# Two layers on one core: the second layer's products with the values gathered into one run for each unit of attention

## The chip, the cores and the metric

The kernel runs on 1 core of one Trainium2 chip. The metric is the device time of one execution in microseconds, as the median of several runs.

## The reference, cut to what matters

Two transformer-like layers work on 1024 tokens of width 1024, all in fp32. The change lies in the second layer, in its attention with a forget gate (16 heads of 64, blocks of 128 queries, causal):

```python
fcum = jnp.cumsum(log_f, axis=-1)
for blk in range(seqlen // ATT_BLOCK):
    q0, q1 = blk * ATT_BLOCK, (blk + 1) * ATT_BLOCK
    s = jnp.einsum('bhqd,bhkd->bhqk', q[:, :, q0:q1], k[:, :, :q1]).astype(jnp.float32) * scale
    s = s + fcum[:, :, q0:q1, None] - fcum[:, :, None, :q1]
    s = jnp.where(kpos[None, :] <= qpos[:, None], s, -jnp.inf)
    prob = jax.nn.softmax(s, axis=-1)
    outs.append(jnp.einsum('bhqk,bhkd->bhqd', prob.astype(v.dtype), v[:, :, :q1]))
...
y_att = (o.astype(f32) * jax.nn.silu(z_att.astype(f32))).astype(x.dtype)
```

Around it stand the projections q, k, v and z_att of the layer's input with the weight `w_in_2`, a state-space branch, two gates, two branch products and an output product.

## The kernel before, in words

**Stages.** The first layer runs first. The second layer opens with projections and the state-space chunks (function `ssd`), and then comes the stage in question: attention, interleaved with the rest of the projections (q, k, v, the attention's gate z, the two branch gates) and with the state-space branch's products. In the profile this stage goes from about 1731 to 2541 us. The attention branch's products, the output product and the last norm follow.

**A unit of attention.** Heads go in pairs p = 0 to 7. Each pair has four units, u = 0 to 3, and a unit has a long and a short block of 128 queries, blocks 7 - u and u, which together always have 9 blocks of keys. A block's keys are taken two at a time; such a step is a *part* (p, i, kp), so that every unit has five parts: four with two blocks of keys and one with a single one. Four functions work on this:

- `scores` (L1551) makes one block's probabilities for one head: GpSimd adds the causal mask to a row of decays (L1560), TensorE multiplies queries and keys (L1568, L1569, tile `S`), VectorE adds and takes the running minimum (L1574), ScalarE takes the exponential (L1580), VectorE the reciprocal (L1582) and the scaling (L1588). Long blocks' probabilities lie in buffers of the pool `pg` (21 buffers of 4 KB for each partition), short ones' in `hp` (9 buffers of 2 KB).
- `tr` (L1594) transposes a part's probabilities for both heads on TensorE into a PSUM tile `pT` (L1600, two buffers), and copies them to a tile `pf` in `hp`: on VectorE for kp = 1 (L87), else on ScalarE (L89).
- `pv` (L1606) multiplies a part with the values (L1617). The two heads' outputs lie at PSUM partitions 0 to 63 and 64 to 127, so that each product takes half of the array's columns. One PSUM tile (`V`, one buffer) holds both of a unit's outputs, at columns 0 and 256. Behind a block's last part VectorE multiplies the output with the gate z (L1626); behind block 3, which is the last of a pair's, SyncE (SP) stores the pair's result to `scr["ya"]` (L1630), and for p = 6 two loads of it follow (`load_T`, L1686).
- `attention` (L1540) sets the order. For each part it issues `tr`; then, as soon as three parts are waiting, the oldest one's `pv`; then one of the four `scores` jobs of the next unit. The list of waiting parts goes on from one unit to the next.

The lines of that loop:

```python
            for i in blocks:
                for kp in range(i // 2 + 1):
                    yield tr(p, i, kp)
                    todo.append((p, i, kp))
                    if len(todo) >= 2 + 1:
                        for _ in range(1):
                            yield pv(*todo.pop(0))
                    if jobs:
                        job = jobs.pop(0)
                        scores(*job)
                        yield 0.107 * (job[1] + 1)
```

**The order around it.** `attention` is a generator; each `yield` gives the TensorE time that the author reckons for what was issued. `interleave` (L255) runs it as the main stream and, after each of its yields, issues batches of the other stream (`until`, L1719: the weight products) until that one has come as far by its own reckoning. A batch is six matmuls of 512 columns (L166, L167, L168, from `gemm_ch`), reckoned as 1.3 us; a task of the other stream is reckoned as 10.5 us, a unit of attention as 6.3 us (L1764 and the lines behind). All other weight products of this stage have the full array's columns (128\*128 in the profile), as have the scores and the transposes. Each engine then works through its queue in order. All loads and stores of this stage go through SP's queue.

Of the kernel before, what the change touches and what calls it, by code (L numbers as in the profile page):

```python
# [10 lines left out]
ALU = mybir.AluOpType  # L11
AX = mybir.AxisListType

P = 128
# [1088 lines left out]
def second_tasks():  # L1103

    tasks = []
    for g in range(4):
        tasks += [("x0", XS + g * 256, g), ("x1", XS + g * 256 + P, g), ("B", BM + g * P, g),
                  ("C", CM + g * P, g), ("z0", Z_SSM + g * 256, g),
                  ("z1", Z_SSM + g * 256 + P, g)]
    gates = [("gate", c0 + m * P, (gi, m)) for gi, c0 in enumerate((GS, GA)) for m in range(8)]  # L1110
    for p in range(8):
        tasks += gates[2 * p - 2 + (p > 5):2 * p + (p > 4) + (p > 5)] if p else []
        tasks += [("q", QO + p * P, p), ("k", KO + p * P, p)]
        if p % 2 == 0:
            tasks += [("v", VO + p * P, (p, ks)) for ks in ((0, 4), (4, 8))]
        tasks += [("za", ZA + p * P, p)]
    return tasks


def second_layer(cx, I, hT, late, scr, out):  # L1120
    nc = cx.nc
    tt = nc.vector.tensor_tensor
# [121 lines left out]
    As = [{} for _ in range(8)]  # L1244
# [295 lines left out]
    def attention():  # L1540

        units = [(p, (7 - u, u)) for p in range(8) for u in range(4)]
        fcs, st, parts, acc = {}, {}, {}, {}

        def load_fc(p):
            for e in range(2):
                fcs[e] = cx.pg("fc")
                h = 2 * p + e
                cx.bcast_row(fcs[e], scr["fc"][h * 8:h * 8 + 8, :].rearrange("c l -> (c l)"))

        def scores(p, i, e):  # L1551
            A = As[p]
            q, kk, kl, fc = A["q"][e], A["kk"][e], A["kl"][e], fcs[e]
            qs = slice(i * P, i * P + P)
            W = (i + 1) * P

            pt = cx.pg("prob") if i > 3 else cx.hp("prob")
            nc.gpsimd.tensor_tensor(out=pt[:, qs], in0=fc[:, qs], in1=cx.pos_q, op=ALU.add)  # L1560
            m = cx.st("m")
            top = BIG
            mi = 0
            for n0 in reversed(range(0, W, 512)):
                n1 = min(W, n0 + 512)
                S = cx.ps("S", "S")
                o = S[:, :n1 - n0]
                nc.tensor.matmul(o, q[:, qs], kk[:, n0:n1], start=True, stop=False)  # L1568
                nc.tensor.matmul(o, q[:, qs], kl[:, n0:n1], start=False, stop=True)  # L1569
                ranges = [(n0, n1, fc)] if n1 < W else [(i * P, W, pt), (n0, i * P, fc)]  # L1570
                for a, z, x in ranges:
                    if a == z:
                        continue
                    nc.vector.tensor_tensor_reduce(  # L1574
                        out=pt[:, a:z], in0=x[:, a:z], in1=S[:, a - n0:z - n0], scale=1.0,
                        scalar=top, op0=ALU.add, op1=ALU.min, accum_out=m[:, mi:mi + 1])
                    top = m[:, mi:mi + 1]
                    mi += 1
            rs = cx.st("rs")[:, 0:1]
            nc.scalar.activation(pt[:, :W], pt[:, :W], AF.Exp, bias=top, scale=-1.0,  # L1580
                                 accum_out=rs)
            nc.vector.reciprocal(rs, rs)  # L1582
            how = "dve"
            if how == "act":
                nc.scalar.activation(pt[:, :W], pt[:, :W], AF.Copy, scale=rs)
            else:
                eng = nc.gpsimd if how == "pool" else nc.vector
                eng.tensor_scalar(out=pt[:, :W], in0=pt[:, :W], scalar1=rs, scalar2=None,  # L1588
                                  op0=ALU.mult)
            st[p, i, e] = pt  # L1590

        def tr(p, i, kp):  # L1594
            t = cx.ps("T", "pT")
            n = min(2, i + 1 - 2 * kp)
            for e in range(2):
                for x in range(n):
                    kt = 2 * kp + x
                    nc.tensor.transpose(t[:, (n * e + x) * P:(n * e + x + 1) * P],  # L1600
                                        st[p, i, e][:, kt * P:(kt + 1) * P], cx.ident)
            f = parts[p, i, kp] = cx.hp("pf")
            cx.evac(f[:, :2 * n * P], t[:, :2 * n * P], kp in (1,))
            return 0.214 * n

        def pv(p, i, kp):  # L1606
            A = As[p]
            if i > 3 and kp == 0:
                acc[0] = cx.ps("V", "o")
            c = 0 if i > 3 else 256  # L1610
            o = acc[0][:, c:c + P]
            f = parts.pop((p, i, kp))
            n = min(2, i + 1 - 2 * kp)
            for x in range(n):
                kt = 2 * kp + x
                for e in range(2):
                    m = nc.tensor.matmul(o[e * 64:e * 64 + 64], A["v"][:, kt, e],  # L1617
                                         f[:, (n * e + x) * P:(n * e + x + 1) * P],
                                         start=kt == 0, stop=kt == i, skip_group_check=True)
                    if kt == 0 and e == 0:  # L1620
                        cx.after(m, acc.get("last"))
            acc["last"] = m
            cx.trail.append(m)
            if 2 * kp + n > i:
                z = A["z"][:, i * P:i * P + P]
                tt(out=z, in0=o, in1=z, op=ALU.mult)  # L1626
                for e in range(2):
                    st.pop((p, i, e))
                if i == 3:
                    nc.sync.dma_start(scr["ya"][p * P:(p + 1) * P, :], A["z"])  # L1630
                    A.clear()
                    if p == 6:
                        load_T(yaT, scr["ya"], 0, [6])
            return 0.269 * n

        todo = []
        jobs = []

        def next_jobs(n):
            p, blocks = units[n]  # L1640
            return [(p, i, e) for i in blocks for e in range(2)]

        load_fc(0)
        for job in next_jobs(0):
            scores(*job)
            yield 0.107 * (job[1] + 1)
        for n, (p, blocks) in enumerate(units):
            if n + 1 < len(units):
                if units[n + 1][0] != p:
                    yield None  # L1650
                    load_fc(p + 1)
                jobs = next_jobs(n + 1)
            for i in blocks:
                for kp in range(i // 2 + 1):
                    yield tr(p, i, kp)
                    todo.append((p, i, kp))
                    if len(todo) >= 2 + 1:
                        for _ in range(1):
                            yield pv(*todo.pop(0))
                    if jobs:  # L1660
                        job = jobs.pop(0)
                        scores(*job)
                        yield 0.107 * (job[1] + 1)
        for a in todo:
            yield pv(*a)

    def segment(gen):
        for dt in gen:
# [17 lines left out]
    def load_T(dst, src, b, ks=range(8)):  # L1686
        for k in ks:
            nc.sync.dma_start(dst(k, b)[1].bitcast(F32), src[k * P:(k + 1) * P, halves[b]])
# [25 lines left out]
    todo = [(kind, what) for kind, _, what in second_tasks()] + [("ssm", m) for m in range(8)]  # L1714
# [46 lines left out]
    interleave((until(marks[0]), 43.0), (chain(delayed(first[1], 1.0), dts), 32.0))  # L1761

    att = attention()
    for n in range(12):  # L1764
        rest = until(marks[n + 1])
# [45 lines left out]
    for n in range(4):  # L1811
        w = cx.weights()
        s = slice(n * 256, n * 256 + 256)
        for i in range(8):
            o = cx.ps("GSGSS"[i % 5], "out2")
# [7 lines left out]
            if n == 3:  # L1823
                ss = cx.st("ss")
                nc.vector.tensor_reduce(out=ss[:, 0:1], in_=sso[:, 4 * i:4 * i + 4], axis=AX.X,
                                        op=ALU.add)
# [103 lines left out]
```

## Time and profile before

| what | value |
|---|---|
| median of 3 runs | 2739.56 us (2738.61 to 2741.25) |
| the profiled execution's own time | 2741.01 us |
| its span, first to last instruction | 2738.9 us |
| TensorE busy (PE) | 2671.0 us |
| VectorE busy (DVE) | 1558.8 us |
| ScalarE busy (ACT) | 1015.2 us |
| GpSimd busy (POOL) | 386.4 us |

PE is TensorE's matmuls, PEld its loads of weights, which overlap with matmuls. Matmuls are pipelined: the next one starts before the one ahead has ended, so that what one costs the queue is read from the starts of neighbours and not from its duration. The bracket at the end of a row of the timeline is the idle time of the engine ahead of it and what ended it; "issue" is a wait for nothing that the profile shows. PEclk is the granted share of TensorE's full clock. A letter q behind an engine's name (SPq) is its instruction queue.

### The profile page before, as it was taken

The page shows a single profiled execution, that of the slowest core. Times are in us where ns is not written, and L with a number is a line of the kernel's source. Part 1 is how long each engine was busy: PE and PEld are TensorE (multiplying, and loading weights), DVE is VectorE, ACT ScalarE, POOL GpSimd, SP SyncE. Part 2 cuts the span into 40 slices and gives each one's busy share as a digit, 9 for nine tenths or more (in the row PEclk, how much of TensorE's full clock was granted, in tenths as well). Part 3 has the DMA queues.
Part 4 walks back from the last instruction along what each step waited for, and adds up shares of the span by engine and source line. Part 5 has one row for each costly group of instructions (what it writes and reads, how often), then busy time and mean ns, then how long its engine had stood idle before and what let it go on. Part 6 is the DMA issues. An engine that isn't in the chain of part 4 may idle for free. (4 is left out here: it accounts for less than half of the span.)

```text
span 2738.9 us, 38386 instructions
## 1 busy us (share of the span) xinstructions
PE 2671.0 (98%) x15391; PEld 2199.6 (80%) x15391; DVE 1558.8 (57%) x2857; ACT 1015.2 (37%) x1753; POOL 386.4 (14%) x368
## 2 busy tenths in 40 slices
PE   5999999999999999999899999999999999999999
PEld 5998667988888888887677778778778778777899
DVE  6645776665555555556577786544544444574443
ACT  4434775152222222233443443433433333352222
POOL 2211211421111100003011222200010000010000
PEclk9999999999999999999999999999999999999999
DMA  7111213321111111121133223222222222253533
GB/s 246 45 55 39 71 42 112 112 74 54 50 52 47 46 47 47 47 56 74 48 103 106 85 87 99 80 75 62 56 76 58 62 89 55 63 195 104 173 125 118
DMA packets 225438, 221.56 MB, mean 81 GB/s; under 512 B 15108, under 2 KB 173420, under 8 KB 225260
## 3 DMA queue, kind: packets, MB, share of 16 engines
q1 hardware_dynamic: 224608, 218.60, 26.0%
q8 instruction: 121, 1.98, 0.3%
q10 hardware_dynamic: 652, 0.51, 0.1%
q14 instruction: 57, 0.47, 0.1%
HBM read 180.67 MB, written 34.21 MB: 78 GB/s over the span
## 5 line engine op out<-in xcount | busy, mean ns | idle before, releaser
L79 ACT CAST wh<-land 128x1024 fp32r<-128x1024 f32 x163 | 170.9, 1050 | 550.5 <-PE up L167 345.1
L81 DVE TENSOR_TENSOR wlo<-land,wh 128x1024 fp32r<-128x1024 f32 x161 | 208.6, 1297 | 278.6 <-ACT wh L79 278.3
L166 PE MATMUL up<-h2h,wh 128*128 128x512 f32 x704 | 274.0, 390 | 0.7 <-DVE y L1022 0.7
L167 PE MATMUL up<-h2l,wh 128*128 128x512 f32 x704 | 274.1, 389 | 0.0
L168 PE MATMUL up<-h2h,wlo 128*128 128x512 f32 x704 | 273.9, 389 | 0.0
L1580 ACT ACTIVATE prob<-prob,m 128x128 f32<-128x128 f32 (+7 forms) x128 | 99.4, 776 | 259.4 <-DVE m L1574 258.8
L1006 DVE TENSOR_TENSOR x<-dn,x 128x512 f32<-128x512 f32 x176 | 119.2, 688 | 75.5 <-PE dn L168 75.5
L166 PE MATMUL ag<-h3h,wh 128*128 128x512 f32 x384 | 161.1, 420 | 0.0
L103 POOL TENSOR_TENSOR rstd<-ms,mhalf 128x1 f32<-128x1 f32 (+3 forms) x58 | 75.9, 1309 | 572.8 <-DVE ms L101 572.8
L1560 POOL TENSOR_TENSOR prob<-fc,consts 128x128 f32<-128x128 f32 x128 | 63.9, 514 | 657.0 <-PE pT L1600 364.3
L89 ACT COPY pf<-pT 128x512 f32<-128x512 f32 (+1 forms) x208 | 114.2, 559 | 112.3 <-PE pT L1600 74.4
L166 PEld LDWEIGHTS up<-h2h,wh 128*128 128x128 f32 x704 | 132.2, 188 | 28.4 <-issue 1.1
L167 PEld LDWEIGHTS up<-h2l,wh 128*128 128x128 f32 x704 | 132.2, 188 | 27.9 <-DVE h2l L228 0.4
L168 PEld LDWEIGHTS up<-h2h,wlo 128*128 128x128 f32 x704 | 132.1, 188 | 27.4
L992 POOL TENSOR_TENSOR wdf<-wdf,gate 128x512 f32<-128x512 f32 x44 | 73.0, 1682 | 568.9 <-DMA wdf<-in_w_down_dram 557.2
L168 PE MATMUL ag<-h3h,wlo 128*128 128x512 f32 x384 | 151.0, 393 | 0.0
L167 PE MATMUL ag<-h3l,wh 128*128 128x512 f32 x384 | 150.7, 392 | 0.0
L166 PE MATMUL dn<-wdh,gh 128*128 128x512 f32 x352 | 138.2, 393 | 1.7 <-DVE x L1006 1.4
L167 PE MATMUL dn<-wdl,gh 128*128 128x512 f32 x352 | 137.3, 390 | 0.0
L168 PE MATMUL dn<-wdh,gl 128*128 128x512 f32 x352 | 137.1, 390 | 0.0
L1574 DVE CUSTOM_DVE_ANT_0 prob<-prob,S 128x128 f32<-128x128 f32 x128 | 36.7, 287 | 175.6 <-PE S L1569 166.5
L166 PE MATMUL tok<-wh,h1h 128*128 128x256 f32 x448 | 130.4, 291 | 2.9 <-ACT h1h L226 2.9
(348 smaller groups left out, 7096.5 us busy)
## 6 DMA issues: line engine op xcount, KB each, us to landing
land<-in_w_in_dram SPq DMA_DIRECT2D x87, 512.0 KB, 3.9
wada<-in_w_ada_dram SPq DMA_DIRECT2D x96, 256.0 KB, 3.5
land<-in_w_up_dram SPq DMA_DIRECT2D x44, 512.0 KB, 4.0
wdf<-in_w_down_dram SPq DMA_DIRECT2D x44, 256.0 KB
scr_g<-gt SPq DMA_DIRECT2D x34, 256.0 KB, 2.3
x<-in_x_dram SPq DMA_DIRECT2D x16, 512.0 KB, 5.7
land<-in_w_out_dram SPq DMA_DIRECT2D x16, 512.0 KB
dab<-scr_da SPq DMA_DIRECT2D x32, 256.0 KB, 4.2
```

What stands on the lines that cost most here:

```text
L79: i = self.nc.scalar.copy(hi, src)
L81: eng.tensor_tensor(out=lo, in0=src, in1=hi.bitcast(F32), op=ALU.subtract)
L89: self.nc.scalar.copy(dst, src)
L103: self.nc.gpsimd.tensor_tensor(out=r[:, :width], in0=t[:, :width], in1=self.mhalf[:, :width], op=ALU.pow)
L166: i = mm(out, lh, rh, start=first, stop=False, **kw)
L167: mm(out, lh, rl, start=False, stop=False, **kw)
L168: self.last = mm(out, ll, rh, start=False, stop=last, **kw)
L992: nc.gpsimd.tensor_tensor(out=f, in0=f, in1=gt2[:, s], op=ALU.mult)
L1006: tt(out=x2[i][:, s], in0=o, in1=x2[i][:, s], op=ALU.add)
L1560: nc.gpsimd.tensor_tensor(out=pt[:, qs], in0=fc[:, qs], in1=cx.pos_q, op=ALU.add)
L1574: nc.vector.tensor_tensor_reduce(out=pt[:, a:z], in0=x[:, a:z], in1=S[:, a - n0:z - n0], scale=1.0, scalar=top, op0=ALU.add, op1=ALU.min, ...
L1580: nc.scalar.activation(pt[:, :W], pt[:, :W], AF.Exp, bias=top, scale=-1.0, accum_out=rs)
```

## The change

The products leave the loop over the parts. A unit now issues its five `tr` with the next unit's `scores` jobs between them, and behind the last one `values` issues all five `pv` of the unit (36 instructions) without a yield between them; then `gated` issues the gate's multiplications for the long and for the short block and, where there is one, the store. One yield with the sum of the reckoned times follows (2.4 us), and only then the interleaving goes on. Nothing is left waiting from one unit to the next. The products, their operands and their PSUM columns are the same.

```diff
--- before.py
+++ after.py
@@ -1621,19 +1621,29 @@
                         cx.after(m, acc.get("last"))
             acc["last"] = m
             cx.trail.append(m)
-            if 2 * kp + n > i:
+            return 0.269 * n
+
+        def gated(p, blocks):
+
+            A = As[p]
+            for i in blocks:
+                c = 0 if i > 3 else 256
                 z = A["z"][:, i * P:i * P + P]
-                tt(out=z, in0=o, in1=z, op=ALU.mult)
+                tt(out=z, in0=acc[0][:, c:c + P], in1=z, op=ALU.mult)
                 for e in range(2):
                     st.pop((p, i, e))
-                if i == 3:
-                    nc.sync.dma_start(scr["ya"][p * P:(p + 1) * P, :], A["z"])
-                    A.clear()
-                    if p == 6:
-                        load_T(yaT, scr["ya"], 0, [6])
-            return 0.269 * n
-
-        todo = []
+            if 3 in blocks:
+                nc.sync.dma_start(scr["ya"][p * P:(p + 1) * P, :], A["z"])
+                A.clear()
+                if p == 6:
+                    load_T(yaT, scr["ya"], 0, [6])
+
+        def values(unit, todo):
+
+            t = sum(pv(*a) for a in todo)
+            gated(*unit)
+            return t
+
         jobs = []
 
         def next_jobs(n):
@@ -1650,19 +1660,14 @@
                     yield None
                     load_fc(p + 1)
                 jobs = next_jobs(n + 1)
-            for i in blocks:
-                for kp in range(i // 2 + 1):
-                    yield tr(p, i, kp)
-                    todo.append((p, i, kp))
-                    if len(todo) >= 2 + 1:
-                        for _ in range(1):
-                            yield pv(*todo.pop(0))
-                    if jobs:
-                        job = jobs.pop(0)
-                        scores(*job)
-                        yield 0.107 * (job[1] + 1)
-        for a in todo:
-            yield pv(*a)
+            todo = [(p, i, kp) for i in blocks for kp in range(i // 2 + 1)]
+            for a in todo:
+                yield tr(*a)
+                if jobs:
+                    job = jobs.pop(0)
+                    scores(*job)
+                    yield 0.107 * (job[1] + 1)
+            yield values((p, blocks), todo)
 
     def segment(gen):
         for dt in gen:
```

## Rows read from the trace of the kernel before

**Rows 1.** The page's head and its part 1, whole program.
```profile
span 2738.9 us, 38386 instructions
...
PE 2671.0 (98%) x15391; PEld 2199.6 (80%) x15391; DVE 1558.8 (57%) x2857; ACT 1015.2 (37%) x1753; POOL 386.4 (14%) x368
```

**Rows 2.** First and last of eight stretches: PE, PEld, DVE, ACT, POOL busy us; PEclk; DMA.
```profile
1740.00:1840.00 100.00, 100.00 (x564) 76.92 (x562) 49.54 (x137) 36.56 (x70) 8.40 (x16) 1.00 0.25 69
...
2440.00:2545.00 105.00, 105.00 (x591) 79.56 (x591) 53.55 (x141) 29.55 (x57) 5.94 (x11) 1.00 0.34 113
```

**Rows 3.** Groups of TensorE's matmuls by shape, 1740 to 2545 us: busy, mean ns, idle.
```profile
L1617 PE MATMUL o<-pf,av 128*64 128x128 f32 x1152 | 99.5, 287 | 0.0
```

**Rows 4.** Who waited for whom, 1740 to 2545 us: us in total, times, longest.
```profile
POOL prob L1560 <- PE o L1617: 77.5, 17, 5.6
...
PEld o L1617 <- issue: 40.5, 129, 0.4
...
DVE prob L1574 <- POOL prob L1560: 7.3, 4, 5.4
```

**Rows 5.** Timeline of TensorE around a group of 8 products: start, us, what, count.
```profile
2000.48 0.39 PE L167 MATMUL gt<-h3l,wh 128*128 128x512 f32 x1
2000.71 0.39 PE L168 MATMUL gt<-h3h,wlo 128*128 128x512 f32 x1
2001.03 0.66 PE L1617 MATMUL o<-pf,av 128*64 128x128 f32 x8
2001.62 0.50 PE L166 MATMUL gt<-h3h,wh 128*128 128x512 f32 x1
2001.96 0.40 PE L167 MATMUL gt<-h3l,wh 128*128 128x512 f32 x1
```

**Rows 6.** Timeline of TensorE around a group of 4 products.
```profile
2023.98 0.40 PE L168 MATMUL gt<-h3h,wlo 128*128 128x512 f32 x1
2024.31 0.44 PE L1617 MATMUL o<-pf,av 128*64 128x128 f32 x4
...
2025.02 0.40 PE L167 MATMUL gt<-h3l,wh 128*128 128x512 f32 x1
```

**Rows 7.** Timeline of TensorE around 16 products of the first stage (L1391).
```profile
1502.46 0.40 PE L168 MATMUL xbc<-h3h,wlo 128*128 128x512 f32 x1
1502.78 0.66 PE L1391 MATMUL Y<-ce,carry 128*64 128x128 f32 x8
1503.27 0.60 PE L1391 MATMUL Y<-seg,xd 128*64 128x128 f32 x8
...
1504.14 0.39 PE L167 MATMUL xbc<-h3l,wh 128*128 128x512 f32 x1
```

**Rows 8.** Timeline of TensorE around four transposes.
```profile
2007.91 0.39 PE L168 MATMUL gt<-h3h,wlo 128*128 128x512 f32 x1
2008.14 0.60 PE L1600 MATMUL pT<-consts,prob 128*128 128x128 f32 x4
...
2008.81 0.39 PE L167 MATMUL gt<-h3l,wh 128*128 128x512 f32 x1
```

**Rows 9.** Timeline: a unit's last transposes and the copy of them.
```profile
2535.55 0.60 PE L1600 MATMUL pT<-consts,prob 128*128 128x128 f32 x4
...
2536.19 0.69 DVE L87 COPY pf<-pT 128x512 f32<-128x512 f32 x1 [1.92 <-PE pT L1600]
```

**Rows 10.** Timelines of TensorE and of VectorE: transposes whose copy came late.
```profile
2438.94 0.49 PE L1600 MATMUL pT<-consts,prob 128*128 128x128 f32 x3
...
2444.87 0.67 DVE L87 COPY pf<-pT 128x512 f32<-128x512 f32 x1
```

**Rows 11.** Timeline of TensorE: a group of 4 split by score products.
```profile
2441.07 0.43 PE L1617 MATMUL o<-pf,av 128*64 128x128 f32 x2
...
2441.80 0.43 PE L1617 MATMUL o<-pf,av 128*64 128x128 f32 x2
```

**Rows 12.** The DMA queue's own waits, 1740 to 2545 us: us in total, times, longest.
```profile
SPq L1630 <- DVE az L1626: 34.1, 8, 8.0
```

## The prediction

> **What bounds the kernel now.** I read the page's busy shares first: TensorE is busy 2671.0 us of a span of 2738.9 us [rows 1]. Busy is a modelled figure there, so I went to the table of stretches for the part that the diff touches, about 1740 to 2545 us: TensorE is busy for the whole of each of the eight stretches of about 100 us, at a granted clock of 1.00 (the upper level, 2.4 GHz), while VectorE has about half of each and ScalarE a third or so [rows 2]. No engine but TensorE can set the end of this stage, so each microsecond that its queue loses there is a microsecond of the program, and the question is only how long its instructions take in the new order.
>
> The groups of matmuls in that stage show 1152 products with the values [rows 3]. That is 36 for each of 32 units: 9 blocks of keys, 2 heads, 2 instructions each. They use half of the array's columns (128\*64), unlike all else in the stage (128\*128). The list of waits has one large entry on TensorE's own side: before these products its weight loads sat idle 129 times, 40.5 us in all, and no other engine is named for it ("issue") [rows 4]. So something is paid each time a group of products begins. Its full price has to be read from start times, as the idle time shows only the side of the loads.
>
> **The price of one group.** An ordinary weight matmul starts 0.23 us after the one before (2000.48 to 2000.71). With a group of 8 products between, 1.25 us pass from the last matmul ahead of it (2000.71) to the second one behind it (2001.96) [rows 5]. Two ordinary steps would be 0.46 us, so the group costs 0.79 us. The extra sits at three places: 0.32 instead of 0.23 us ahead of the group, 0.34 instead of 0.23 us behind it, and a fixed part inside it. For a group of 4 the same reckoning gives 2025.02 - 2023.98 - 0.46 = 0.58 us [rows 6]; for a run of 16 in the first stage of this layer, in the same shape of 128\*64 with 128 columns streamed, 1504.14 - 1502.46 - 0.46 = 1.22 us [rows 7]. From 8 to 16 the slope is 0.43/8 = 0.054 us for each product, from 4 to 8 it is 0.21/4 = 0.053. What is left is the same each time: 0.79 - 0.43 = 0.36 us by the pair 8 and 16, 0.79 - 0.42 = 0.37 by the pair 4 and 8. I take 0.36 us, since the longer run is nearer to what comes.
>
> **Part 1, the products in one run.** Before, a unit has 5 groups (four of 8 products, one of 4): 160 in all. After, it has one run of 36: 32 in all. 128 fixed prices go: 128 x 0.36 = 46 us. Instructions, their operands and their number stay. A run of 36 is not in the trace; if its pace were 0.052 instead of 0.054, a further 2 us would go, and the other side is a rival below. I take 0.054, as it did not change from 4 to 16.
>
> **Part 2, transposes and score products.** They keep their order and number; only the products between them leave. Four transposes between weight matmuls cost 2008.81 - 2007.91 - 0.46 = 0.44 us [rows 8], 0.11 each and no fixed price that could be saved or added, so I count 0. They fall closer together on TensorE by one group (0.8 us) out of some 5 us for a part; two PSUM buffers take them, and a copy out of one takes 0.69 us [rows 9]. Bound: nothing to 0.1 us for each of 160 parts if the copies lagged; the weight matmuls between them cover it.
>
> **Part 3, the last part of a unit.** Before, the products ran two parts behind their transposes. Now the last part's products end the run that begins right behind its transposes. From the transposes' start to the end of the copy took 2536.19 + 0.69 - 2535.55 = 1.33 us on VectorE [rows 9]. The cover is 4 transposes (0.44) and at least 28 products (28 x 0.054 = 1.5), 1.9 us, plus six weight matmuls (1.4 us) where one more batch is due. So the copy is ready 0.6 us early: 0. Where VectorE had a backlog, a copy came late: transposed from 2438.94, copied only by 2444.87 + 0.67 = 2445.54 us, 6.6 us [rows 10]. Met at the end of a run, this would stall TensorE 6.6 - 1.9 = 4.7 us, or break the run if other matmuls are put in its place. I expect five of the 32 runs to be broken once or to wait as long: 5 x 0.36 = 2 us back. Both ends: 0 and 32 x 0.36 = 12 us.
>
> **Part 4, gating, the store and the buffers.** The 64 multiplications with the gate stay; a unit's two now wait for its whole run. Behind them in VectorE's queue stand the next unit's minima and copies, and for those TensorE has a unit's worth of weight matmuls, so 0. The 8 stores of `ya`, and the two loads for the pair p = 6 behind one of them, stand behind the gates in SP's queue as before, where the store waited 34.1 us in all [rows 12]. Each now leaves at the end of its unit instead of two parts into the next one, so nothing queued behind it on SP, the weight loads above all, comes later. The long blocks' probabilities are free after their transposes, as before. In the `hp` pool five copies live until the run, where three did, with four short probability tiles: nine, all that the pool has. It fits without a spare; that nobody waits is the assumption that the rival below drops.
>
> **The sum.** The profiled execution took 2741.0 us, 2.1 us more than its span and 1.45 us over the median of 2739.56. 2741.0 - 46 + 2 = 2697.0 us; against the median 2695.5 us.
>
> **A rule against it.** In the run of 16 the first eight are through in 1503.27 - 1502.78 = 0.49 us, the way in included, and the second eight add no more than 0.43 us, 0.054 each [rows 7]. The Trainium skill ("TensorE: Matmul & The Clock Gate", section "Back-to-back issue gap") says that a long stream of load and matmul pairs with 128 columns settles at about 81 ns for each matmul. By that, 36 products take 36 x 0.027 = 1.0 us more than I count, and the sum would be about 2727 us; a cause of that kind is rival (b). The trace speaks against it up to 16 products; a longer run no row here shows.
>
> **The rivals.** (a) *The runs break.* A run broken in two pays one more fixed price, as in the group of 4 split by score products at 2441.07 and 2441.80 us [rows 11]. If each of the 32 does, 32 x 0.36 = 12 us come back: about 2705 us. For it: the last copy has 0.6 us to spare and in the stretch near 2440 us none. Against: the groups that I followed are almost all whole. (b) *The pace falls in a long run.* If products beyond the 16 that were seen went at the transposes' 0.11 us [rows 8], 20 x 0.056 = 1.1 us a unit would be given back, 36 us in all: 2729 us with no broken runs beside it. Against: a slope that is the same twice. (c) *The run is not formed*: weight matmuls still come between the parts, because the order within TensorE's queue lets ready work pass. Then nothing changes: 2739 us. Against: before, nearly every group of 8 stayed together. (d) *Slower: the short blocks' tiles.* With nine of nine `hp` buffers in use, GpSimd's first write into a short block's probabilities has to wait for a run of products. That wait exists already: 17 times, 77.5 us, 4.6 us on average, and four times VectorE stood behind GpSimd, 7.3 us [rows 4]. It would have to delay TensorE by over 46/32 = 1.4 us a unit to eat the gain; at 4.6 us each, 32 x 4.6 = 147 us against 46 saved gives about 2840 us. Against: those tiles are needed nearly a unit (some 25 us) after the run that frees their buffers, and TensorE has weight matmuls to do meanwhile.
>
> **How the numbers follow.** The forecast (32 runs, a few broken) gets 0.73, (a) 0.15, (b) 0.05, (c) 0.03, (d) 0.04. The measurement of this kernel can tell 0.2%, 5.5 us, from no change. Faster is the forecast with (a) and (b), 0.93; no difference is (c), 0.03; slower is (d), 0.04. The low end takes a fixed price of 0.37 us, the pace of 0.052 and no broken run: 2739.6 - 47.4 - 2 = 2690, and 2 us for the stages that are merely re-timed: 2688 us. The high end takes (a) with the worst wait of 4.7 us at the end of one run and 2 us of re-timing: 2712 us.
>
> **What would show it.** Right: the stretches stay full on TensorE at clock 1.00 and the stage's end moves forward by about 44 us. The products come in groups of 36 that take 36 x 0.054 + 0.36 = 2.3 us from matmul to matmul, and the entry "issue" before them falls from 129 times to about 32. (a) shows as groups of 28 or 32 with a remnant behind weight matmuls, or as idle TensorE time released by a copy; (b) as groups of 36 that last over 3 us; (c) as groups of 8; (d) as idle time of TensorE released by a probability tile, with GpSimd waiting for products in each unit. I am wrong in the main step if the runs are whole and the stage is no shorter.

## The result, and the profile after

The changed kernel takes 2695.3 us in the median of four runs (2694.76 to 2696.34), the kernel before 2739.09 us in four runs on the same chip. The ratio is 0.9841, with a 95% interval of 0.9824 to 0.9858: 43.8 us less. The forecast was 2695.5 us.

The page's head and its part 1, whole program, which answer to [rows 1]:

```profile
span 2693.0 us, 38385 instructions
...
PE 2626.4 (98%) x15391; PEld 2208.2 (82%) x15391; DVE 1547.2 (57%) x2857; ACT 1014.4 (38%) x1753; POOL 391.3 (15%) x368
```

The number of matmuls is the same, 15391, and TensorE's busy time has fallen by 44.6 us. The span is 45.9 us shorter. To see where, take two landmarks: the first transpose of the attention (L1600) and the output product of the last stage. (The first product with the values is no landmark: the change itself moves it behind all five transposes of its unit.) Each line has the first and last start ahead of the shape; first the transposes, in the kernel before and then in the changed one (view by tile, `pT`):

```profile
L1600 PE MATMUL pT<-consts,prob x576: 270/272/330, 1731.4 to 2535.9; 128*128 128x128 f32 x192
```

```profile
L1600 PE MATMUL pT<-consts,prob x576: 270/272/328, 1730.1 to 2484.3; 128*128 128x128 f32 x192
```

The same for the output product (view by tile, `out`):

```profile
L166 PE MATMUL out<-wh,mergedh x256: 277/283/283, 2640.2 to 2732.0; 128*128 128x256 f32 x128
```

```profile
L166 PE MATMUL out<-wh,mergedh x256: 278/283/283, 2594.3 to 2686.1; 128*128 128x256 f32 x128
```

It starts 45.9 us earlier and lasts 91.8 us in both, so nothing was gained or lost from there on. The transposes start 1.3 us earlier, ahead of everything that the change touches. What is left, 44.6 us, was gained between the two landmarks, in the stage that the change touches and the branch products behind it.

Two of the stretches of that stage in the changed kernel (columns as in [rows 2]):

```profile
1740.00:1840.00 100.00, 100.00 (x595) 83.14 (x594) 51.72 (x154) 40.64 (x78) 10.35 (x18) 1.00 0.27 77
2340.00:2440.00 100.00, 100.00 (x590) 81.99 (x589) 68.32 (x182) 49.91 (x95) 9.91 (x15) 1.00 0.48 159
```

TensorE is as full as before and at the same clock of 1.00, but 595 of its matmuls begin in the first stretch, where 564 did. "Busy all the time" stood in both profiles; the lost time was inside it.

The group of products with the values, and the waits that answer to [rows 3, 4], from 1740 to 2500 us:

```profile
L1617 PE MATMUL o<-pf,av 128*64 128x128 f32 x1152 | 71.5, 276 | 0.0
```

```profile
POOL prob L1560 <- PE o L1617: 177.0, 30, 21.1
...
DVE prob L1574 <- POOL prob L1560: 9.3, 5, 3.1
...
PEld o L1617 <- issue: 8.7, 31, 0.4
```

The same 1152 instructions cover 71.5 us, where they covered 99.5. The idle entry "issue" ahead of them has fallen from 129 times and 40.5 us to 31 times and 8.7 us. GpSimd waits for the products longer than before, 177.0 us against 77.5, and for the transposes shorter, 278.3 us against 364.3, so in part it may be the same idle time under another name. It costs nothing so far, as VectorE stood behind GpSimd for 9.3 us in five waits (7.3 in four before).

And one run of 36 in the timeline of TensorE:

```profile
2000.19 0.39 PE L168 MATMUL gt<-h3h,wlo 128*128 128x512 f32 x1
2000.51 2.19 PE L1617 MATMUL o<-pf,av 128*64 128x128 f32 x36
2002.62 0.50 PE L166 MATMUL gt<-h3h,wh 128*128 128x512 f32 x1
2002.96 0.39 PE L167 MATMUL gt<-h3l,wh 128*128 128x512 f32 x1
```

From 2000.19 to 2002.96 less two ordinary steps (0.46) it costs 2.31 us. Four groups of 8 and one of 4 cost 4 x 0.79 + 0.58 = 3.74 us before [rows 5, 6].

In the order of TensorE's instructions, the 1152 products stood in 163 groups before and stand in 37 now: 30 whole runs of 36 and seven pieces of two units. The program issues 32 whole runs; the order in which the compiled program gives them to TensorE breaks two. The price of a group, from all groups that have weight matmuls of 512 columns on both sides, has a median of 0.351 us: about 0.10 on the way in, 0.15 inside, 0.11 on the way out.

### The profile page after: what moved, and what is told of

The parts are those of the page before. It is cut to its first block, busy times and chain, and to the rows that moved or that the text cites. A ratio compares the mean times of both kernels' runs of the same rounds, so it can differ in the third digit from the quotient of the medians.

```text
span 2693.0 us, 38385 instructions
## 1 busy us (share of the span) xinstructions
PE 2626.4 (98%) x15391; PEld 2208.2 (82%) x15391; DVE 1547.2 (57%) x2857; ACT 1014.4 (38%) x1753; POOL 391.3 (15%) x368
## 5 line engine op out<-in xcount | busy, mean ns | idle before, releaser
L1560 POOL TENSOR_TENSOR prob<-fc,consts 128x128 f32<-128x128 f32 x128 | 68.6, 555 | 635.1 <-PE pT L1600 278.3
L168 PE MATMUL tok<-wh,h1l 128*128 128x256 f32 x448 | 128.7, 288 | 0.8 <-DVE h1l L228 0.8
```

What stands on the lines that cost most here:

```text
L168: self.last = mm(out, ll, rh, start=False, stop=last, **kw)
```

## The experiments

The theory (A): each time TensorE goes from products of the full array to products of half its columns and back costs about 0.35 us, whatever the number of products between. The rivals: the gates and the store (B), any new group whatever its shape (D), the order alone (E), a slower pace in long runs (F), the full pool of buffers (G).

### Two runs for each unit

```diff
-            todo = [(p, i, kp) for i in blocks for kp in range(i // 2 + 1)]
-            for a in todo:
+            for i in blocks:
+                todo = [(p, i, kp) for kp in range(i // 2 + 1)]
+                for a in todo:
...
-            yield values((p, blocks), todo)
+                yield values((p, (i,)), todo)
```

> The changed kernel, but a unit's products in two runs: the long block's behind its own transposes, the short block's behind its own. Theory A (each time TensorE goes from products of the full array to products of half its columns and back costs 0.36 us, however many products follow): 64 runs instead of 32, so 32 x 0.36 = 11.5 us more than the changed kernel's 2695.3: about 2707 us, 32 us under the kernel before. Rival B (the gain comes from the gates: the short block's products no longer wait for the long block's gate on the same PSUM tile, and the gates and the store stand together): that order is back here, so about 2739 us.

Measured: 2711.25 us, ratio 0.9897 (0.9883 to 0.9910), 16 us over the changed kernel. That is 4 us more than expected, mostly because the compiled order broke more of the runs: 78 pieces stand in its timeline, not 64. 41 more than in the changed kernel at 0.351 us make 14.4 us. B, which wanted 2739, is out here.

### The gates and the store alone

```diff
-            if 2 * kp + n > i:
-                z = A["z"][:, i * P:i * P + P]
-                tt(out=z, in0=o, in1=z, op=ALU.mult)
-                for e in range(2):
-                    st.pop((p, i, e))
+            if i < 4 and 2 * kp + n > i:
+                for b, cb in ((7 - i, 0), (i, 256)):
+                    z = A["z"][:, b * P:b * P + P]
+                    tt(out=z, in0=acc[0][:, cb:cb + P], in1=z, op=ALU.mult)
+                    for e in range(2):
+                        st.pop((p, b, e))
```

> The kernel before with its 160 groups, but the two gates of a unit and the store stand together behind the unit's last products, as in the changed kernel. Theory A: still 160 groups, so no gain, 2739 us within 4 us. Rival B (gates and store are the gain): about 2695 us.

Measured: 2738.51 us, ratio 0.9995 (0.9986 to 1.0004), with 161 groups in the timeline. No gain: the place of the gates and of the store is worth nothing by itself. B is out a second time.

### Products on the full array, in both orders

```diff
                 for e in range(2):
-                    m = nc.tensor.matmul(o[e * 64:e * 64 + 64], A["v"][:, kt, e],
+                    m = nc.tensor.matmul(acc[0][:, c + e * P:c + e * P + P],
+                                         A["v"][:, kt].rearrange("p h d -> p (h d)"),
                                          f[:, (n * e + x) * P:(n * e + x + 1) * P],
-                                         start=kt == 0, stop=kt == i, skip_group_check=True)
+                                         start=kt == 0 and e == 0, stop=kt == i,
+                                         skip_group_check=True)
...
-                tt(out=z, in0=o, in1=z, op=ALU.mult)
+                for e in range(2):
+                    h = slice(e * 64, e * 64 + 64)
+                    tt(out=z[h], in0=acc[0][h, c + e * P:c + e * P + P], in1=z[h], op=ALU.mult)
```

> The order of the kernel before, but each product has the values of both heads as its weights, 128 columns, so that it takes the full array like all else in the stage; half of each output is not used, and a gate becomes two half-height ones. Full-array products can't run side by side: by the transposes' pace 0.11 us each, 36 x 0.11 = 3.96 us a unit without a price per group, against 4 x 0.79 + 0.57 = 3.73 us now. Theory A (the price is that of changing between full and half array): 32 x 0.23 = 7 us slower than before, about 2746 us. Rival D (any new group of products pays, by its PSUM tile, its number format or its operands): 3.96 + 5 x 0.36 = 5.76 us a unit, 65 us slower, about 2804 us.

> The order of the changed kernel with the same full-array products. Theory A: with no change of shape to save, one run or five make no difference, so the same as the full-array kernel in the order of before, within 6 us (about 2746 us). Rival D: 128 prices of 0.36 us are saved here too, 46 us less than that kernel (about 2758 us if it has 2804).

Measured: 2750.09 us (ratio 1.0038, 1.0025 to 1.0051) in the order of before, 2748.95 us (1.0035, 1.0021 to 1.0048) in the order of the change. The two are the same: with full-array products the change is worth nothing. D wanted 2804 and 2758.

A group of 8 of the first, in TensorE's timeline, and the idle entry of its loads (waits in the stage):

```profile
2000.76 0.39 PE L168 MATMUL gt<-h3h,wlo 128*128 128x512 f32 x1
2000.99 1.05 PE L1617 MATMUL o<-pf,av 128*128 128x128 f32 x8
2001.80 0.48 PE L166 MATMUL gt<-h3h,wh 128*128 128x512 f32 x1
2002.11 0.39 PE L167 MATMUL gt<-h3l,wh 128*128 128x512 f32 x1
```

```profile
PEld o L1617 <- issue: 0.2, 1, 0.2
```

And a run of 36 of the second:

```profile
1997.45 0.39 PE L168 MATMUL ag<-h3h,wlo 128*128 128x512 f32 x1
1997.69 4.18 PE L1617 MATMUL o<-pf,av 128*128 128x128 f32 x36
2001.62 0.48 PE L166 MATMUL ag<-h3h,wh 128*128 128x512 f32 x1
2001.94 0.40 PE L167 MATMUL ag<-h3l,wh 128*128 128x512 f32 x1
```

The way in is an ordinary step of 0.23 us. By the same reckoning the 8 cost 2002.11 - 2000.76 - 0.46 = 0.89 us and the 36 cost 4.03 us, 0.11 each and nothing for the group; "issue" is down to one time. With the number format, the PSUM tile and the operands' tiles left as they were, the price went with the shape. (The shape is the share of the array, the width of the weights and the half of the output's partitions at once; these runs do not separate them.) [rows 7] agrees: there two groups of 8 of the same half-array shape, with different operands, stand directly behind each other and pay once. The 32 x (36 x 0.111 - 3.74) = 8 us that the slower products cost are about what the totals show (10.5). The Trainium skill ("TensorEngine Tiling (Array Packing)", section "Key Properties") says that a change of the tiling mode, other than a change of the tile, drains TensorE. These two runs agree in so far as no group pays where the shape stays the same; that what the others pay for, 0.35 us there and back, is a drain, no trace here shows.

### Nine groups for each unit

```diff
-        def pv(p, i, kp):
+        def pv(p, i, kp, xs):
...
             for x in range(n):
+                if x not in xs:
+                    continue
...
+                    if len(todo) >= 2:
+                        yield pv(*todo[0], (0,))
                     yield tr(p, i, kp)
                     todo.append((p, i, kp))
                     if len(todo) >= 2 + 1:
-                        for _ in range(1):
-                            yield pv(*todo.pop(0))
+                        last = todo.pop(0)
+                        if min(2, last[1] + 1 - 2 * last[2]) > 1:
+                            yield pv(*last, (1,))
```

> The kernel before, but a part's products in two groups with the next part's transposes between them, so that a unit has nine groups of four instead of five. Theory A (0.35 to 0.36 us for each group, whatever its length): 288 groups instead of 160, 128 x 0.35 = 45 us slower than before, about 2784 us. Rival E (the gain of the changed kernel came from its order, products behind the transposes, and not from the number of groups): about 2739 us.

Measured: 2775.41 us, ratio 1.0127 (1.0111 to 1.0142): 35.7 us slower, not 45. E is out. The groups in the timeline are 275, so 112 prices of 0.35 us would be 39 us. The rest is in the neighbours: 82 of these groups stand directly ahead of transposes, 71 more than in the kernel before, as this one does:

```profile
1900.04 0.28 PE L168 MATMUL ag<-wh,h3l 128*128 128x256 f32 x1
1900.25 0.44 PE L1619 MATMUL o<-pf,av 128*64 128x128 f32 x4
1900.62 0.66 PE L1600 MATMUL pT<-consts,prob 128*128 128x128 f32 x4
1901.04 0.48 PE L166 MATMUL ag<-h3h,wh 128*128 128x512 f32 x1
```

Four transposes take 1901.04 - 1900.62 = 0.42 us behind a group. Behind a weight matmul, in the kernel before, they take 2008.50 - 2008.14 = 0.36 us:

```profile
2008.14 0.60 PE L1600 MATMUL pT<-consts,prob 128*128 128x128 f32 x4
2008.50 0.48 PE L166 MATMUL gt<-h3h,wh 128*128 128x512 f32 x1
```

The way out costs 0.06 us there instead of 0.11, and 71 x 0.05 = 3.6 us less brings 39 down to about what was measured.

### Each product twice in its run

```diff
-                for e in range(2):
+                for e in (0, 1, 0, 1):
+                    again = acc.get("now") == (i, kt)
...
-                                         start=kt == 0, stop=kt == i, skip_group_check=True)
+                                         start=kt == 0 and not again,
+                                         stop=kt == i and again, skip_group_check=True)
...
+                    if e == 1:
+                        acc["now"] = (i, kt)
```

> The changed kernel with each product made twice, so that a run has 72 (the outputs are then twice as large). Theory A (0.0545 us each in a run of any length): 32 x 36 x 0.0545 = 63 us more than 2695, about 2758 us. Rival F (a long run settles at a slower pace, 0.081 us by the Trainium skill's page on TensorE, or 0.11 as the transposes): 93 us more for the added half alone, about 2788 us, or 127 us more, about 2822 us.

Measured: 2763.37 us, ratio 1.0076 (1.0058 to 1.0093), 68 us over the changed kernel, of which 5 lie ahead of the stage (its first product begins at 1751.4 instead of 1746.2 us). A run of 72 in the timeline:

```profile
2001.93 0.40 PE L168 MATMUL ag<-h3h,wlo 128*128 128x512 f32 x1
2002.25 4.15 PE L1618 MATMUL o<-pf,av 128*64 128x128 f32 x72
2006.33 0.50 PE L166 MATMUL ag<-h3h,wh 128*128 128x512 f32 x1
2006.67 0.39 PE L167 MATMUL ag<-h3l,wh 128*128 128x512 f32 x1
```

2006.67 - 2001.93 - 0.46 = 4.28 us against 2.31 us for 36: 1.97/36 = 0.0547 us for each added product, the pace of the short groups. F is out.

### Two more buffers

```diff
-        with cx.pool("all", act=32, wl=2, wp=4, pg=21, hp=9, ge=5):
+        with cx.pool("all", act=32, wl=2, wp=4, pg=20, hp=11, ge=5):
```

> The changed kernel with eleven instead of nine buffers in the pool of the copies and short probability tiles, and twenty instead of twenty-one in the pool of the large tiles. Theory A (GpSimd's longer waits for the products cost nothing, as TensorE never waits for a probability tile): the same as the changed kernel, 2695 us within 4. Rival G (the full pool eats a part of the gain, by late probability tiles or by broken runs): 2685 us or less.

The two more are small ones; one large buffer is given up for them. Measured: 2718.66 us, ratio 0.9918 (0.9903 to 0.9932), 23 us slower than the changed kernel, which neither side expected. What became of the wait in question, in the stage:

```profile
POOL prob L1560 <- PE o L1617: 6.6, 7, 1.9
```

GpSimd's wait for the products is nearly gone (177.0 us in the changed kernel), and TensorE gained nothing by it: the runs are the same 37, and from the first to the last product the stage takes 743.4 us (1765.4 to 2508.8) against 741.6. So G is out for the stage itself. The loss lies ahead of it, 19 us by the first product, around the change from the first layer to the second. This stretch in this run's kernel, then in the changed one:

```profile
1260.00:1400.00 140.00, 113.94 (x502) 89.73 (x502) 84.26 (x136) 54.76 (x86) 27.05 (x23) 0.87 0.20 67
```

```profile
1260.00:1400.00 140.00, 125.99 (x597) 99.61 (x596) 87.50 (x162) 61.51 (x98) 27.84 (x24) 0.96 0.23 73
```

TensorE idles 12 us more there, in waits of its transposes (L205) for VectorE, and the granted clock of the stretch is 0.87 instead of 0.96. The longest of these waits, which the changed kernel does not have there:

```profile
PE tr L205 <- DVE ms L101: 11.5, 4, 4.7
```

One large buffer fewer is what this run had other than the two small ones more; that it is the cause was not tried by itself.

### The first layer too, and the changed kernel again

```diff
-                if len(todo) >= 2 + 4:
-                    for _ in range(4):
+                if len(todo) >= 2 + 8:
+                    for _ in range(8):
...
-        while at_done[0] < 17:
+        while at_done[0] < 19:
...
-        while at_done[0] < 26:
+        while at_done[0] < 28:
```

> The changed kernel, and in the first layer's attention too the products with the values are gathered: eight parts (32 products of 256 columns, half the array) behind their transposes instead of four (16), with the two counts that start the work behind them raised from 17 and 26 to 19 and 28. Theory A: the 512 products stand in 66 runs in the trace of the changed kernel; if 16 to 40 runs remain, 26 to 50 prices of 0.35 us go, 9 to 17 us: about 2680 to 2686 us. Against it: in that stage VectorE has 39 of 50 us busy, so that TensorE may wait instead, or the runs may break as often as before: then 2695 us or a little more.

> The changed kernel once more, on the same chip as the run before: 2695 us within 3 by every theory.

Measured on one chip: 2689.57 us (ratio 0.9813, 0.9799 to 0.9826; 2686.82 to 2691.65) with the first layer too, 2696.65 us (0.9838, 0.9824 to 0.9851; 2695.69 to 2697.65) without. It is the fastest kernel of this study, by some 7 us. It is no proof of theory A, though: the products of the first layer stand in 61 pieces instead of 66, so the order was broken again, and five prices, if one is the same for 256 columns, are worth 1.8 us. The first product of the next stage (`up`) begins 6.2 us earlier, at 552.7 us. Of that, 1.8 us were there when that layer's attention began its transposes (241.5 us instead of 243.3), ahead of what the edit touches; where in the attention the other 2.6 us come from stays open.

## Why the prediction was right

**The price of a group.** It was read as 0.36 us from three places in one trace and is 0.351 in the median. That it belongs to the change of shape, which the prediction only supposed from 128\*64 beside 128\*128, is shown by the two full-array kernels: without the change of shape there is no price, and no gain from gathering. The totals follow the number of groups, with slopes of 0.39, 0.33 and 0.32 us for each. The 95% intervals of the ratios, some 4 us to either side, make that 0.09, 0.04 and 0.04 us either way, so the slopes do not contradict 0.351:

| groups in the timeline | time, us | kernel |
|---|---|---|
| 37 | 2695.3 | changed |
| 78 | 2711.25 | two runs a unit |
| 163 | 2739.1 to 2740.1 | before |
| 275 | 2775.41 | nine groups a unit |

**Part 1** stands: 126 groups fewer, at 0.351 us 44.2 us, against 44.6 us between the landmarks and 43.8 us between the medians. The pace in a long run, 0.0547 us, is the one that was taken, and it holds up to 72 products. The Trainium skill's 81 ns for each matmul ("TensorE: Matmul & The Clock Gate", section "Back-to-back issue gap"), from which the prediction worked out about 2727 us, does not hold here, where products of half the array took 54.7 ns each.

**Part 2** stands by the table of waits: no copy of transposes shows up as a wait of TensorE's products.

**Part 3**, the last part, was right in its size and half right in its cause. Five broken runs were expected; there are five pieces more than units, but they come from two units only. One unit was cut into five pieces where VectorE and ScalarE were behind, as [rows 10] had suggested. TensorE's products there, and what VectorE and then ScalarE did meanwhile:

```profile
2389.82 0.65 PE L1617 MATMUL o<-pf,av 128*64 128x128 f32 x6
...
2391.27 0.66 PE L1617 MATMUL o<-pf,av 128*64 128x128 f32 x8
...
2397.79 0.65 PE L1617 MATMUL o<-pf,av 128*64 128x128 f32 x6
...
2399.49 0.66 PE L1617 MATMUL o<-pf,av 128*64 128x128 f32 x8
...
2401.44 0.66 PE L1617 MATMUL o<-pf,av 128*64 128x128 f32 x8
```

```profile
2390.63 7.31 DVE L1700 TENSOR_TENSOR ysTl<-ysTl,ysTh 128x512 fp32r<-128x512 f32 x12
...
2399.67 0.68 DVE L87 COPY pf<-pT 128x512 f32<-128x512 f32 x1
```

```profile
2389.65 4.25 ACT L1699 CAST ysTh<-ysTl 128x512 fp32r<-128x512 f32 x8
2393.80 0.37 ACT L89 COPY pf<-pT 128x256 f32<-128x256 f32 x1
```

On VectorE twelve splits of the state-space branch (7.31 us), on ScalarE eight of their casts (4.25 us) stand ahead of the copies, and the last copy ends at 2400.35 us. The other unit was cut in two with twelve weight matmuls between, though all its copies were done:

```profile
2252.89 0.60 PE L1600 MATMUL pT<-consts,prob 128*128 128x128 f32 x4
2253.58 0.59 ACT L89 COPY pf<-pT 128x512 f32<-128x512 f32 x1 [0.41 <-PE pT L1600]
...
2254.84 1.09 PE L1617 MATMUL o<-pf,av 128*64 128x128 f32 x14
...
2257.47 1.52 PE L1617 MATMUL o<-pf,av 128*64 128x128 f32 x22
```

The last copy ended at 2254.17, ahead of the first product. This cut is in the order that TensorE was given and not in a wait; why it was given so was not tried. The same seven pieces stand in the traces of the last three kernels (two more buffers, the first layer too, the changed one again), so the five pieces of the first unit, too, belong to the compiled order; that the late copies made it so fits their times but was not tried. That the sum of these pieces came out at the 2 us that were put down is partly luck. So is the agreement of 2695.5 with 2695.3 us: the four medians of the kernel before alone lie 1.0 us apart, and 1.3 us of the profile's gain lie ahead of the stage, where the prediction had nothing.

**Part 4** stands: the gates and the store are worth nothing (the run with them alone), and the full pool of buffers makes GpSimd wait without TensorE waiting. (For the pair p = 6 one load follows the store, not two; nothing hung on it.) Rival (d) had its wait growing as described, from 77.5 to 177.0 us, and never reached the point from which it decides. Rival (a) is there in two units of 32, (b) is out by the runs of 36 and 72, (c) by the count.

## What to carry to other kernels

An engine that is busy all the time can still lose time: take the starts of an instruction's neighbours with and without it, and see whether the cost has a part that does not grow with its number. Here a change between full-array and half-array products costs 0.35 us there and back, so half-array products belong together in one run, as long as the copies that they read are ready and the buffers hold them. Count the groups in the new profile: the compiled order breaks runs that the program has whole, and the time follows the count.

## What the runs showed of the hardware that was not expected

Two half-array products of 128 columns run side by side: inside a run of 36 the two of a pair start 5 to 7 ns apart, and the next pair 109 ns later. So one costs 0.0547 us, a full-array one of the same length 0.111 us, and a half-array group has to have about (0.35 / 0.056) 6 products before it is the cheaper form. The groups measured agree: 4 products cost 0.58 us in the half-array form and 0.45 us in the full-array kernel, 8 cost 0.79 and 0.89 us. A product is here a row of the trace; each matmul of the program that takes part is two of them (18 matmuls, 36 rows a unit). The way out of half-array products is about half as dear into transposes (0.06 us) as into weight matmuls of 512 columns (0.11 us). And the kernel with two small buffers more and one large one of 21 fewer lost 19 us far from the stage that was studied.
